# Batch norm over a matmul: the weight's first blocks loaded as two pairs, and chunk 0 multiplied in two passes over half of k

## The chip, the cores and the metric

One core of a Trainium2 chip runs the kernel. The core has five engines with an instruction queue each: TensorE (PE; its weight loads are shown apart as PEld), VectorE (DVE), ScalarE (ACT), GpSimd (POOL) and SyncE (SP). DMA transfers are issued by POOL and SP and are carried out by 16 DMA engines. The metric is the time on the device of one execution in microseconds (us); less is better.

## The reference

```python
x: (16, 512, 1024) float32;  weight: (1024, 768) float32;  gamma, beta: (768,)
y = np.matmul(x, weight)
mean = np.mean(y, axis=(0, 1), keepdims=True)
var = np.var(y, axis=(0, 1), keepdims=True)
y_norm = (y - mean) / np.sqrt(var + eps)
return (gamma * y_norm + beta).astype(np.float32)
```

Mean and variance go over all 8192 rows of y, so a column's output can be written only when that column is known for every row.

## The kernel before

**Tiling.** The 8192 rows of x are 16 chunks of 512 rows (`CH`, index c). k (1024) is cut into `JW` = 4 blocks (index jw 0 to 3), each of 2 x 128 in the contraction (index e). The 768 columns are 6 tiles of 128 (nt). The first two tiles (`GA` = 2, 256 columns) are computed by rows: x is the stationary operand and w moves ("rows", `rows_unit`, `mm_rows`, line 493). The other four are computed by columns: w is stationary and x moves ("columns", `col_unit`, `mm`, line 558).

**Loading.** POOL issues all loads of x and w, with a cast from float32 to bfloat16. One load of x (`load_x`, line 392) is four DMAs, one for each quarter of k; chunks 0 and 1 are loaded in halves of 256 rows (four DMAs of 128 KB, as they land), later chunks whole (four of 256 KB). One load of w (`load_w`, line 383) is four DMAs too, each for 32 of the 128 partitions, of the blocks jw to jw1: 96 KB for one block, 192 KB for two. A DMA from POOL takes one of eight lanes in turn, and its issue waits until the lane's previous DMA has landed. Before the loop SP reads a few bytes of w's block 0 (line 345).

**Turning x.** x arrives with rows along the partitions' free side in 32 x 32 blocks, and VectorE transposes it (`turn_x`, line 421; line 414 for the chunks in `SINGLE`). For chunk 0 each half of 256 rows is turned in two steps, first for the blocks 0 and 1 of k, then for 2 and 3; the other chunks in one step for each half.

**Order of the work.** The kernel makes a list of tasks with due times (`t` for loads, `clock[0]` for TensorE) and estimated durations for each engine. `arrange` (line 122) then simulates the engines, the DMA lanes and the buffers with these estimates, and fixes in which order each engine's instructions stand. So a change of an estimate or of one task can change the order on all engines. The list of the first loads is at line 426; the estimate for a w load is at line 437.

**TensorE's start.** `wake` (line 570) is work that computes nothing that is used. `wake(WAKE)` is eight float32 matmuls of width 512 and `SMALL` = 22 small bfloat16 matmuls of width 128 (line 577); `wake(FILL)` is `FILL` = 2 of the float32 ones (line 574). `part(q0, q1, jws)` (line 757) does rows and columns of chunk 0 for the half-chunks q0 to q1 and the blocks jws of k. What is done before the change, in this order: the first idle work; the first half-chunk with block 0; two idle matmuls; the second half-chunk with block 0; both halves with block 1; then both with the blocks 2 and 3, the rows by `rows_unit` and the columns by `col_unit` (lines 768 to 771). After that chunk 1 and the following chunks come with all of k at once. The sums go on in PSUM from one part to the next: two banks for rows, four for columns.

**After that.** Up to about 57 us TensorE does rows and columns of the chunks 1 to 3; then rows almost alone up to about 96 us, the rest of the first two column tiles (line 798) up to 106 us, and the columns of nt 2 to 5 of the remaining chunks until 190 us. ScalarE squares a rows' result (line 642) and copies it (line 655), VectorE (line 645) and POOL or VectorE (line 649) add up sums and squares. Normalized output is stored by SP from about 105 us on.

Of the kernel before, what the change touches and what calls it, by code (L numbers as in the profile page):

```python
# [227 lines left out]
def kernel(  # L228
# [27 lines left out]
    JW = KQ // 64  # L256
    PIECES = ((0,QR),(QR,QR))
    WAKE = 8
    FILL = 2
    SMALL = 22  # L260
    TOUCH = 1
    EARLY = 4
    SHORT = 2
# [27 lines left out]
    def seq(bi):  # L291

        ins = bi.ins
        prev = last.get(ins.engine)
        if prev is not None:
            tc.add_manual_dep(
                ins, prev,
                mybir.DependencyInfo(mybir.DependencyClass.NoSync, mybir.DependencyReason.DATA),
                reason="order",
            )  # L300
        last[ins.engine] = ins.name
        return bi
# [48 lines left out]
    def task(prio, engines, emit, deps=(), lock=False, **kw):  # L351
        t = Task(prio, engines, emit, deps, **kw)
        t.lock = lock
        tasks.append(t)
        return t

    def dve(occ):
        return {"DVE": (occ, occ + 0.09)}

    def act(occ):  # L360
        return {"ACT": (occ, occ + 0.11)}
# [14 lines left out]
    w_ready, x_ready, x_slot, plain, last_loads = {}, {}, {}, {}, []  # L376

    def load_w(jw, jw1):
        def emit(eng):
            rows = weight.rearrange("(i jw c e) n -> i c jw (e n)", i=4, jw=JW, e=2)  # L380
            dst = w_sb.rearrange("p jw e n -> p jw (e n)")
            for i in range(4):
                seq(nc.gpsimd.dma_start(dst[32 * i:32 * i + 32, jw:jw1], rows[i, :, jw:jw1]))
        return emit

    def load_x(m0, rows, slot):
        def emit(eng):
            x_bf = piece(slot).bitcast(bf16).rearrange("p (t k) -> p t k", k=KQ)
            slot.tile = x_bf
            src = x_flat[m0:m0 + rows].rearrange("(t r) k -> r t k", r=32)  # L390
            for i in range(4):
                bi = seq(nc.gpsimd.dma_start(x_bf[32 * i:32 * i + 32], src[:, :, KQ * i:KQ * (i + 1)]))  # L392
            slot.loader.ins = bi.ins
        return emit
# [8 lines left out]
    def turn_x(xslot, slot, m0, t0, jw0, jw1, new, rows=QR):  # L403
        def emit(eng):
            single = m0 // CH in SINGLE
            if new:
                xT_sb = xtpool.tile([P, JW, 2, CH] if single else [P, JW, CH, 2], bf16, tag="xT")
                slot.tile = xT_sb
            half, row = divmod((m0 + 32 * t0) % CH, QR)
            if single:  # L410
                src = xslot.tile[:, t0:t0 + rows // 32].rearrange("p t (jw c e) -> p t jw e c", jw=JW, e=2)
                dst = slot.tile[:, :, :, half * QR + row:half * QR + row + rows]
                dst = dst.rearrange("p jw e (t r) -> p t jw e r", r=32)
                seq(nc.vector.transpose(dst[:, :, jw0:jw1], src[:, :, jw0:jw1]))  # L414
                return
            src = xslot.tile[:, t0:t0 + rows // 32].rearrange("p t k -> p (t k)").bitcast(f32)
            src = src.rearrange("p (t jw c) -> p t jw c", jw=JW, c=32)
            dst = slot.tile.rearrange("p jw m e -> p (jw m e)").bitcast(f32)
            dst = dst.rearrange("p (jw q t r) -> p q t jw r", jw=JW, q=QPC, r=32)
            dst = dst[:, half, row // 32:(row + rows) // 32, jw0:jw1]  # L420
            seq(nc.vector.transpose(dst, src[:, :, jw0:jw1]))  # L421
        return emit

    for c in range(C):
        x_slot[c] = Slot(xts)
    order = [("x", 0), ("w", 0, 1)] + [("x", 1), ("w", 1, 2), ("w", 2, 4)]
    order += [("x", q) for q in range(2, SHORT * QPC)] + [("c", c) for c in range(SHORT, C - 1)]
    at = M - CH
    for rows in (CH-P,P):
# [2 lines left out]
    t = 1.0  # L432
    affine = None
    for kind, n, *n1 in order:
        if kind == "w":
            took = 4 * 192 * 4 * (n1[0] - n) / 4 * PER_KB * 1.024
            w_ready[n] = task(t, {"POOL": (2.0, 2.0)}, load_w(n, *n1), dma=took)
            w_ready[n].count = 4
            t += 2.1 * (n1[0] - n)
            if n1[0] == JW:  # L440
                idt = task(t, {"POOL": (0.6, 0.6)}, lambda eng: make_identity(nc, ident))
                task(t, act(0.25), lambda eng: seq(nc.scalar.copy(ident32, ident)), [idt])
            continue
        rows = n1[0] if kind == "p" else QR if kind == "x" else CH
        m0 = n if kind == "p" else n * rows
        if m0 == M // 2:
            affine = task(t, {"SP": (5.0, 7.0)}, load_affine, [x_ready[m0 // CH - 3, 0, JW]])
        slot = Slot(rings, rows // 32 * KQ // 2)
        load = task(
            t, {"POOL": (2.68 * rows / CH, 2.68 * rows / CH)}, load_x(m0, rows, slot), dma=rows * K * 4 / 1024 * PER_KB * 1.024,  # L450
            takes=[slot])
        load.count = 4
        slot.loader = load
        last_loads.append(load)
        t += 2.7 * rows / QR
        for i in range(rows // QR):
            c, q = divmod(m0 // QR + i, QPC)
            for j0, j1 in ((0, JW // 2), (JW // 2, JW)) if m0 < CH else ((0, JW),):
                new = q == 0 and j0 == 0
                x_ready[c, q, j1] = task(  # L460
                    -1000 + t, dve((2.2 if c in SINGLE else 1.16) * (j1 - j0) / JW + 0.02),
                    turn_x(slot, x_slot[c], m0, i * QR // 32, j0, j1, new), [load],
                    uses=[slot] if new else [slot, x_slot[c]], takes=[x_slot[c]] if new else [])
                if not new:
                    x_ready[c, q, j1].deps.append(x_ready[c, 0, JW // 2 if m0 < CH else JW])
            x_ready.setdefault((c, q, JW // 2), x_ready[c, q, JW])
        if rows % QR:
            t0 = rows // QR * QR // 32
            m1 = m0 + 32 * t0
            c, q = divmod(m1 // QR, QPC)  # L470
            x_ready["tile", m1 // P] = task(
                -1000 + t, dve(0.63), turn_x(slot, x_slot[c], m0, t0, 0, JW, False, P),
                [load, x_ready[c, 0, JW]], uses=[slot, x_slot[c]])
            x_ready[c, q, JW] = x_ready[c, q, JW // 2] = x_ready["tile", m1 // P]
# [95 lines left out]
    def wake(count, slot):  # L570
        def emit(eng):
            idle_ps = psum.tile([P, CH], f32, tag="b")
            for _ in range(count):
                seq(nc.tensor.matmul(idle_ps, idle_sb[:, 0:P], idle_sb, start=True, stop=True))  # L574
            small = idle_sb[:, 0:P // 2].bitcast(bf16)
            for _ in range(SMALL if count == WAKE else 0):
                seq(nc.tensor.matmul(idle_ps[:, 0:P], small, small, start=True, stop=True))
        return emit
# [5 lines left out]
    def pe_task(occ, emit, deps, key=None, **kw):  # L584
        t = task(clock[0], pe(occ), emit, deps, **kw)
        t.after = begun.get(key)
        begun[key] = t if key else None
        emit.task = t
        clock[0] += occ
        return t  # L590
# [7 lines left out]
    def rows_unit(c, ts, jws=range(JW)):  # L598
        key = "row", c, ts[0]
        slot = bank_of.setdefault(key, None) or Slot(banks)  # L600
        bank_of[key] = slot
        kw = {"takes": [slot], "uses": [x_slot[c]]} if jws[0] == 0 else {"uses": [slot, x_slot[c]]}
        h = ts[0] * P // QR
        t = pe_task(0.873 * len(ts) * len(jws) / JW, mm_rows(c, ts, list(jws), slot),
                    waits(jws, c, h, h + 1), key, **kw)
        if jws[-1] == JW - 1:
            rows_stats(c, ts, slot, t)
        return t
# [148 lines left out]
    def part(q0, q1, jws):  # L757
        for h in range(q0, q1):
            rows_unit(0, [2 * h, 2 * h + 1], jws)
        for nt in range(GA, NT):  # L760
            col_unit(nt, 0, jws, q0, q1)

    part(0, 1, [0])
    fill_slot = Slot(banks)
    pe_task(0.87 * FILL, wake(FILL, fill_slot), [w_ready[0]], takes=[fill_slot])
    part(1, 2, [0])
    part(0, 2, [1])
    for h in range(2):
        rows_unit(0, [2 * h, 2 * h + 1], [2, 3])
    for nt in range(GA, NT):  # L770
# [500 lines left out]
    for c, r0, rows in ends:  # L1271
        due = E + 2.0 + 0.6 * c
        n = max(rows // CH, 1)
# [30 lines left out]
    order = arrange(tasks, turns)  # L1304
# [39 lines left out]
```

## Time and profile before

| | us |
|---|---|
| runs (three) | 208.77, 208.78, 208.35; median 208.77 |
| span of the profiled execution, first to last instruction | 206.5 |
| TensorE busy in it | 191.4 (93 %) |
| VectorE busy | 156.3 (76 %) |
| ScalarE busy | 139.8 (68 %) |
| POOL busy | 132.0 (64 %) |
| granted clock of TensorE, mean | 0.985 |

The profile page lists a busy time for each engine, then the span in slices, then the chain of work that ended last: from the last instruction it is followed back, at each step to what released it. On the chain, lines 558 and 493 (columns and rows) have 51 % and 23 % of the span, loads of x 5 % and loads of w 3 %. TensorE's busy time is no measure of how full it is, since matmuls overlap; more is told by what it waited for. The profiled execution's own time is not listed apart from its span; the runs' median is 2.27 us above the span.

A line of the timeline is: start, length, engine, line of the kernel, operation, output<-inputs, shape, how many, and in brackets the idle time before it and what ended it. A line of the windows is: the stretch, its length, then busy time and number of instructions of PE, PEld, DVE, ACT and POOL, the granted clock, the DMA engines' share and what they wrote in GB/s. A line of the waits is: who waited <- for whom, us in total, times, longest.

### The profile page before, as it was taken

How to read it: one execution, taken by the hardware profiler on the slowest of the kernel's cores; microseconds unless marked ns; L12 is line 12 of the kernel's file. 1: busy time of each engine (PE TensorE's matmuls, PEld its weight loads, DVE VectorE, ACT ScalarE, POOL GpSimd, SP SyncE). 2: the span in 40 equal slices, each digit the busy share in tenths (PEclk: the TensorE clock that was granted, in tenths of full speed). 3: DMA queues.
4: the chain of work that ended last, by engine and by line, in shares of the span. 5: the costliest groups of instructions: out<-in, count | busy, mean ns of one | idle time of the engine just before them, and what ended most of it. 6: DMA issues, size and time to landing. Idle time of an engine off the chain costs nothing.

```text
span 206.5 us, 3506 instructions
## 1 busy us (share of the span) xinstructions
PE 191.4 (93%) x1211; PEld 116.3 (56%) x1226; DVE 156.3 (76%) x238; ACT 139.8 (68%) x248; POOL 132.0 (64%) x148
## 2 busy tenths in 40 slices
PE   7998999999999999999999999999999999996900
PEld 3465564747488888777875444444444445553600
DVE  4220779999999999968989998977999648947900
ACT  2000560369989999998978767997376776866950
POOL 7877964877488999999304999599954440440000
PEclk9999999999999999999999999999999999999995
DMA  5999999999999999999676898999999999999898
GB/s 55 169 168 193 192 196 196 196 198 197 190 193 197 197 197 195 196 197 195 110 120 199 311 339 307 267 350 307 315 317 245 291 325 308 274 341 347 254 347 243
DMA packets 98497, 48.73 MB, mean 236 GB/s; under 512 B 24240, under 2 KB 97968, under 8 KB 98480
## 3 DMA queue, kind: packets, MB, share of 16 engines
q0 software_dynamic: 34688, 18.36, 65.1%
q1 hardware_dynamic: 63792, 30.16, 52.8%
q8 instruction: 9, 0.15, 0.3%
q14 instruction: 8, 0.07, 0.1%
HBM read 36.71 MB, written 25.17 MB: 300 GB/s over the span
## 4 chain that ended last, share of the span: by engine, by line
PE 82%; DMA 8%; ACT 3%; issue 1%; POOL 1%; DVE 1%; ACTq 0%; POOLq 0%
PE y_ps L558 51%; PE y_ps L493 23%; DMA ring<-in_x_dram 5%; PE y_ps L798 4%; ACT o_sb L1293 3%; DMA w_sb<-in_weight_dram 3%; PE o_ps L1028 2%; PE a_ps L887 1%; POOL ring L392 1%; PE y_ps L736 1%; PE o_ps L1058 0%; ACTq L1339 0%; PE tot_ps L855 0%; DVE fin L743 0%; ACT y_sb L746 0%
## 5 line engine op out<-in xcount | busy, mean ns | idle before, releaser
L558 PEld LDWEIGHTS <-w_sb 128*128 128x128 bf16 x512 | 49.7, 97 | 57.4
L558 PE MATMUL y_ps<-x_pl,w_sb 128*128 128x512 bf16 x256 | 60.5, 379 | 0.3
L392 POOL DMA_DIRECT2D ring<-in_x_dram x76 | 47.5, 630 | 13.0 <-DVE xT_sb L414 5.0
L558 PE MATMUL y_ps<-xT_sb,w_sb 128*128 128x512 bf16 (+1 forms) x241 | 55.1, 376 | 0.4
L493 PE MATMUL y_ps<-w_sb,xT_sb 128*128 128x256 bf16 x448 | 50.7, 273 | 0.6 <-DMA w_sb<-in_weight_dram 0.6
L493 PEld LDWEIGHTS <-xT_sb 128*128 128x128 bf16 x448 | 43.6, 98 | 8.3 <-issue 1.7
L421 DVE STREAM_TRANSPOSE xT_sb<-ring 128x1024 f32<-128x1024 f32 (+1 forms) x29 | 31.2, 1111 | 12.4 <-DMA ring<-in_x_dram 12.2
L694 DVE BATCH_NORM_STATS2 stats<-y_ps 128x6 f32<-128x512 f32 x46 | 30.9, 687 | 12.7 <-PE y_ps L558 12.5
L698 ACT CAST y_sb<-y_ps 128x512 bf16<-128x512 f32 x51 | 29.4, 590 | 14.5 <-DVE stats L694 12.4
L926 POOL TENSOR_TENSOR ring<-ring,sum 128x1024 f32<-128x1024 f32 (+1 forms) x11 | 23.7, 2193 | 14.6 <-DVE ring L921 14.5
L649 POOL TENSOR_TENSOR sum<-sum,sq_sb 128x512 f32<-128x512 f32 x21 | 26.9, 1281 | 3.2 <-ACT sq_sb L642 2.1
L642 ACT ACTIVATE sq_sb<-y_ps 128x512 f32<-128x512 f32 x28 | 16.3, 607 | 18.0 <-PE y_ps L493 17.1
L645 DVE TENSOR_TENSOR sum<-y_ps,sum 128x512 f32<-128x512 f32 x28 | 18.9, 675 | 9.1 <-ACT sq_sb L642 7.8
L530 ACT COPY x_pl<-xT_sb 128x1024 bf16<-128x1024 bf16 x24 | 24.4, 1052 | 1.7 <-DVE xT_sb L421 1.7
L655 ACT CAST y_sb<-y_ps 128x512 bf16<-128x512 f32 x28 | 16.0, 599 | 7.8 <-DVE sum L645 7.6
L530 POOL COPY x_pl<-xT_sb 128x1024 bf16<-128x1024 bf16 x15 | 16.1, 1108 | 8.0 <-DVE x_pl L530 5.2
L921 DVE TENSOR_TENSOR ring<-y_sb,a_ps 128x1024 f32<-128x1024 bf16 (+1 forms) x16 | 16.7, 1080 | 0.3 <-DMA out_dram<-ring 0.3
L1139 POOL TENSOR_TENSOR ring<-ring,sum 128x1024 f32<-128x1024 f32 x4 | 9.6, 2412 | 11.0 <-DVE ring L1135 11.0
L1193 ACT CAST ring<-ring 128x1024 f32<-128x1024 bf16 x15 | 15.7, 1049 | 1.0 <-DMA ring<-y_sb 1.0
L1028 PE MATMUL o_ps<-ident,y_sb 128*128 128x128 bf16 x104 | 14.2, 221 | 2.2 <-DVE y_sb L1280 2.0
L414 DVE STREAM_TRANSPOSE xT_sb<-ring 128x2048 bf16<-128x2048 bf16 x6 | 13.5, 2289 | 0.2 <-DMA ring<-in_x_dram 0.2
L574 PE MATMUL idle_ps<-idle_sb 128*128 128x512 f32 x20 | 11.2, 717 | 1.5 <-DVE idle_sb L314 1.5
(97 smaller groups left out, 155.0 us busy)
## 6 DMA issues: line engine op xcount, KB each, us to landing
out_dram<-ring SPq DMA_DIRECT2D x38, 512.0 KB, 3.7
ring<-in_x_dram POOLq DMA_DIRECT2D x52, 256.0 KB, 8.8
out_dram<-o_sb SPq DMA_DIRECT2D x6, 512.0 KB, 4.9
ring<-in_x_dram POOLq DMA_DIRECT2D x16, 128.0 KB, 5.3
out_dram<-ring SPq DMA_DIRECT2D x4, 256.0 KB, 3.0
w_sb<-in_weight_dram POOLq DMA_DIRECT2D x8, 96.0 KB, 5.1
w_sb<-in_weight_dram POOLq DMA_DIRECT2D x4, 192.0 KB, 5.9
ring<-in_x_dram POOLq DMA_DIRECT2D x4, 192.0 KB, 8.1
```

The lines of the kernel that those rows point to most:

```text
L392: bi = seq(nc.gpsimd.dma_start(x_bf[32 * i:32 * i + 32], src[:, :, KQ * i:KQ * (i + 1)]))
L421: seq(nc.vector.transpose(dst, src[:, :, jw0:jw1]))
L493: seq(nc.tensor.matmul(y_ps[:, s], x_of(c, jw, e, t * P, (t + 1) * P), w_sb[:, jw, e, 0:NA], start=(s == 0 and jw == 0 and e == 0), stop=( ...
L530: seq(nc.scalar.copy(dst, pairs) if eng == "ACT" else ENG[eng].tensor_copy(dst, pairs))
L558: seq(nc.tensor.matmul(y_ps, w_sb[:, jw, e, nt * P:(nt + 1) * P], moving(c, jw, e, q0 * QR, q1 * QR, parted), start=(jw == 0 and e == 0 an ...
L645: seq(nc.vector.tensor_add(sum1, slot.tile[:, 0:n], sum1))
L649: seq(ENG[eng].tensor_add(acc, acc, state["sq"][:, 0:n]))
L694: seq(nc.vector.bn_stats(dst, slot.tile))
L698: seq(nc.scalar.copy(y(nt, c), slot.tile))
L921: seq(nc.vector.tensor_mul(slot.o, y_row[c].y[:, s0:s1], aff[0][:, None, :].to_broadcast([P, n, NA])))
L926: seq(ENG[eng].tensor_add(slot.o, slot.o, row[:, None, :].to_broadcast([P, n, NA])))
L1028: seq(nc.tensor.transpose(dst, src, ident))
```

## The change

```diff
-    FILL = 2
-    SMALL = 22
+    FILL = 1
+    SMALL = 34
...
-    order = [("x", 0), ("w", 0, 1)] + [("x", 1), ("w", 1, 2), ("w", 2, 4)]
+    order = [("x", 0), ("w", 0, 2), ("x", 1), ("w", 2, 4)]
...
-            w_ready[n] = task(t, {"POOL": (2.0, 2.0)}, load_w(n, *n1), dma=took)
+            w_ready[n] = task(t, {"POOL": (2.14, 2.14)}, load_w(n, *n1), dma=took)
...
-    part(0, 1, [0])
+    part(0, 1, [0, 1])
     fill_slot = Slot(banks)
     pe_task(0.87 * FILL, wake(FILL, fill_slot), [w_ready[0]], takes=[fill_slot])
-    part(1, 2, [0])
-    part(0, 2, [1])
+    part(1, 2, [0, 1])
```

w comes in two loads of four DMAs instead of three: the blocks 0 and 1 between the two halves of chunk 0, and the blocks 2 and 3 after them as before. Chunk 0 then takes two passes over k for its first half of k: the first half-chunk with the blocks 0 and 1, and the second half-chunk with the same; the blocks 2 and 3 follow for both, as before. The columns of block 1, once eight matmuls of width 512, become sixteen of width 256. Twelve small idle matmuls are added before the first pass, and one of the two idle matmuls between the passes is gone. The planner's estimate of POOL's time for a w load goes from 2.0 to 2.14 us.

In the order that the planner then fixes, TensorE's instructions after chunk 0 and SP's are as before. On POOL, VectorE and ScalarE some instructions of the row phase stand otherwise: one add of squares goes from POOL to VectorE, POOL has one add more ahead of the loads of chunks 10 and 11, VectorE turns chunk 9 before an add instead of after it, and ScalarE has squares and copies of three rows' results in another order.

## Prediction
> **What bounds the kernel now.** I read the chain of waits first, then the waits of TensorE, then its timeline in the stage that the diff touches, then the rates of the DMA engines. The chain's columns are start, length, what.
>
> ```profile
> 8.65 4.67 DMA ring<-in_x_dram
> 13.32 0.28 issue
> 13.61 6.00 DMA w_sb<-in_weight_dram
> 19.61 0.14 issue
> 19.74 1.91 PE y_ps L493 x16
> 21.65 3.62 PE y_ps L558 x16
> 25.26 3.67 PE y_ps L493 x32
> ```
>
> Up to 19.74 us the chain is loading: the last quarter of x's second half-chunk lands at 13.32, and frees the lane on which the last quarter of w's blocks 2 and 3 is issued (13.61); that lands at 19.61. From 19.74 on the chain is TensorE, almost without a break. TensorE's own waits (total, times, longest) say the same:
>
> ```profile
> PE o_ps L1028 <- DVE y_sb L1280: 2.0, 1, 2.0
> PE idle_ps L574 <- DVE idle_sb L314: 1.5, 1, 1.5
> PE y_ps L493 <- DMA w_sb<-in_weight_dram: 0.6, 1, 0.6
> ```
>
> Of these, the first is the closing stage and the second the start; between lies one wait, on w. So the change is worth what it moves the moment 19.74, provided that nothing later takes it back.
>
> The stage itself on TensorE:
>
> ```profile
> 10.67 1.39 PE L577 MATMUL idle_ps<-idle_sb 128*128 128x128 bf16 x22
> 12.33 1.07 PE L558 MATMUL y_ps<-xT_sb,w_sb 128*128 128x256 bf16 x8
> 13.24 1.88 PE L574 MATMUL idle_ps<-idle_sb 128*128 128x512 f32 x4
> 16.30 1.03 PE L493 MATMUL y_ps<-w_sb,xT_sb 128*128 128x256 bf16 x8
> 17.40 1.74 PE L558 MATMUL y_ps<-xT_sb,w_sb 128*128 128x512 bf16 x7
> ```
>
> Start to start this gives prices: a small idle matmul (11.89 - 10.67) / 22 = 0.0555 us; a row matmul 0.109 (16 from 19.74 to 21.48); a 512-wide column matmul 0.2255 (16 from 21.48 to 25.10); a 256-wide column matmul (13.24 - 12.33) / 8 = 0.114; an idle matmul of line 574 two passes, together (14.96 - 13.24) / 2 = 0.86.
>
> **The loads, piece by piece.** The view of the two loading lines, asked issue by issue, gives issue and time to landing. x's first half lands until 8.37. Block 0 of w (issued from 3.73, 5.0 to 5.1 each) lands at 8.8 to 10.26, 0.48 apart. x's second half lands at 10.9, 11.6, 12.3, 13.32; block 1 at 14.4, 14.9, 15.3, 15.8; the pair 2 and 3 at 16.8, 17.7, 18.7, 19.61. In step, a quarter of one w block takes 0.48, of x 0.68, of a pair 0.94: 4 x 0.48 + 4 x 0.68 + 4 x 0.48 + 4 x 0.94 = 10.32, so from 8.37 the end would be 18.69. It was 19.61. The missing 0.92 lies in two steps: x's last quarter (1.03 instead of 0.68) and block 1's first (1.07 instead of 0.48). The rates by window (last number, GB/s) show the same dip:
>
> ```profile
> 12.00:15.00 3.00, 3.00 (x19) 1.78 (x16) 1.30 (x2) 0.00 (x0) 1.81 (x4) 1.00 1.04 155
> 15.00:19.60 4.60, 4.08 (x28) 2.57 (x27) 0.00 (x0) 0.00 (x0) 3.70 (x7) 1.00 1.14 197
> 30.00:80.00 50.00, 49.89 (x367) 35.81 (x367) 48.09 (x54) 37.47 (x60) 39.39 (x50) 1.00 1.49 196
> ```
>
> The late quarters also had a short time from issue to landing (4.7, 5.2); the pair's had 5.6 to 6.1 and all came on time. So the queue may have been too shallow there. It may also be the reads of a fresh block of w that were slow; the page can't say.
>
> **The change, part by part.**
>
> *POOL's queue.* Eight issues of single blocks (0.50 each) become four of a pair (0.53, as the pair's from 11.21): the first w load ends at 3.73 + 4 x 0.53 = 5.85 instead of 5.71. Behind it stand the two identity operations (0.23, 0.31) and x's second half. Its first issue slips from 5.84 to 6.0, the second likewise; the third and fourth wait for landings of x's first half (7.66, 8.37) and stay at 7.94 and 8.65. Cost nothing: x's data now stand behind a pair that lands until 12.1. The second pair takes the lanes of the first, so it is issued some 0.28 after each of its landings, 9.6 to 12.4. Behind these waits on POOL stand only the loads of chunk 1, whose data follow the pair's anyway.
>
> *Landings.* 8.37 + 4 x 0.94 = 12.13 for blocks 0 and 1; + 4 x 0.68 = 14.85 for x; + 4 x 0.94 = 18.61 for blocks 2 and 3. Each of these last eight would have about 6.2 from issue to landing. Best case 1.00 earlier than 19.61; worst of the plain cases, the 0.92 recurs and it is 0.08 earlier. I take the best, since leads of 5.6 and more came on time in this stage, and keep both.
>
> [...]
>
> *TensorE.* Twelve more small idle matmuls: real work begins at 10.67 + 34 x 0.0555 = 12.56, not 11.89; w is there at 12.13. First pass, 8 rows and 16 columns: 0.87 + 1.82 = 2.69, to 15.25. One idle matmul less: 0.86, to 16.11. x's second half is turned for k's first half by 14.85 + 0.13 + 0.65 + 0.1 = 15.73, so no wait. Second pass 2.69, to 18.80. In all the same work: 16 columns of 0.114 stand for 8 of 0.2255. The pair is usable 0.13 after landing, 18.74. So blocks 2 and 3 begin at 18.80 instead of 19.74, with the same 32 matmuls still to do: **0.94 earlier**; 0.05 with the late pieces.
>
> *Later stages.* x's loads run at 196 GB/s without a pause, so the whole stream moves with the pair, 1.00. It must, for late in the row phase both meet (chunk 12):
>
> ```profile
> 84.91 2.37 DVE L421 STREAM_TRANSPOSE xT_sb<-ring 128x1024 f32<-128x1024 f32 x2 [0.23 <-DMA ring<-in_x_dram]
> 86.25 0.75 PEld L493 LDWEIGHTS <-xT_sb 128*128 128x128 bf16 x6
> ```
>
> The first transpose ends 1.25 after 84.91, at 86.16; TensorE loads it at 86.25. It can gain 0.09 more than the loads do and no more. The built order also moves work behind this: on POOL one more add of squares (1.28) stands ahead of the loads of chunks 10 and 11, on VectorE one more (0.68) between the transposes of chunks 9 and 10. Chunk 11 is issued at 68.27 with 7.1 to landing; 5.8 is left, and 5.1 to 5.6 was enough for the last x loads. VectorE's is hidden by the waits of 0.23 (chunk 12) and 1.59 (chunk 13) on loads; uncovered it costs 0.68 - 0.23 = 0.45. I take nothing for both, and 0.19 for slips of the kind already there: 32 row matmuls of chunk 1 took 3.67, of chunk 2 3.49.
>
> *Sum.* 0.94 - 0.19 = 0.75. The profiled span is 206.5, to become 205.75; the median of the runs, 208.77, lies 2.27 above the span: **208.0**.
>
> **The rivals.**
>
> *The lateness comes again once* (a fresh block of w is slow to read, wherever it stands). For: the dip ends with block 1. Against: block 0 came on time behind x. Gain 0.05 to 0.4, about **208.6**.
>
> *It comes twice, and the kernel is slower.* Place: the landing of either pair; price 0.92 each. Then blocks 2 and 3 land at 18.61 + 1.84 = 20.45, TensorE starts 0.84 later: **209.6**. It decides from 1.00 of lateness in all. For: the step to block 1 is the only one where w came late, and both pairs now begin with such a step. Against: the pair at 15 to 19.6 ran at 197 GB/s.
>
> *TensorE's clock falls back*, since fewer idle matmuls stand between. That there are two speeds is seen in the first idle matmuls, at equal granted clock:
>
> ```profile
> 5.07 0.33 PEld L574 LDWEIGHTS idle_ps<-idle_sb 128*128 128x128 f32 x1 [0.52 <-issue]
> 5.92 0.22 PEld L574 LDWEIGHTS idle_ps<-idle_sb 128*128 128x128 f32 x1 [0.52 <-issue]
> 6.38 0.19 PEld L574 LDWEIGHTS idle_ps<-idle_sb 128*128 128x128 f32 x1 [0.24 <-issue]
> ```
>
> 0.85 from one to the next, then 0.43, after 4.4 us of work. At half speed for as long, half the work is lost: +2.2, about **210.2**. Against: the pause of 0.6 before 19.74 left the row matmuls at 0.109, and the worst new pause is under 1 us (x late by 0.9: 16.1 to 16.6, and another before the second pair). [...]
>
> **How the numbers follow.** Forecast 0.52 (own range 207.7 to 208.45), late once 0.25, late twice 0.14, clock 0.05, the moved adds 0.04 (208.5 to 209.5). The first two and the near edge of the third make the range 207.6 to 209.0. The measurement tells 0.2 %, 0.42 us: faster means below 208.35. Faster: 0.9 of the forecast and a tenth of late once, 0.50. Slower: late twice, clock, most of the moved adds and a little of the rest, 0.25. Same: 0.25.
>
> **What would show it.** Right: the wait on w before line 493 shrinks from 0.60 to under 0.1 and ends by 18.9; the rate from 12 to 15 us is near 195; the second pair lands by 18.7; x of chunk 12 is turned about 1 us earlier. Wrong: a rate near 155 again at some place before 16 us (late once, or twice); row matmuls at twice 0.109 after a pause (clock); an early start whose gain is gone at chunk 12, with a new wait of TensorE on line 421 (moved adds).

## The result, and the profile after

| | before | after |
|---|---|---|
| median of 10 runs each (lowest to highest), us | 207.88 (207.39 to 208.78) | 209.12 (208.78 to 209.85) |
| span of the profiled execution, us | 206.5 | 207.1 |

The ratio after to before is 1.005, 95 % interval 1.0031 to 1.0068: the changed kernel is slower by about 1 us. The three runs that the prediction started from (208.35 to 208.78) are among the ten of the kernel before, and among its four slowest; the other seven have a median of 207.79. The kernel before also differs from one group of experiments to the next (207.94 to 208.30), so from here on a run is compared by its ratio to the runs of the kernel before that stand beside it.

At chunk 0 nearly all came as predicted. The chain of waits of the changed kernel (start, length, what), from the small idle matmuls to the blocks 2 and 3:

```profile
11.02 1.90 PE idle_ps L577 x34
12.92 0.87 PE y_ps L493 x8
13.80 1.81 PE y_ps L558 x16
15.61 0.86 PE idle_ps L574 x2
16.47 0.87 PE y_ps L493 x8
17.34 1.81 PE y_ps L558 x16
19.15 1.75 PE y_ps L493 x16
```

No load stands on it any more; TensorE goes from one piece into the next and begins the blocks 2 and 3 at 19.15 on this chain. A piece of the chain starts only where the one before it ends; by the timeline, which the prediction used, the first pass starts at 12.76 and the blocks 2 and 3 at 18.99. Before, they started at 19.74 in both views. The waits of TensorE are down to the start and the closing stage:

```profile
PE o_ps L1027 <- DVE y_sb L1279: 2.0, 1, 2.0
PE idle_ps L574 <- DVE idle_sb L314: 1.5, 1, 1.5
```

The windows over the loading (the last number is GB/s) have no dip: 206 where it was 155.

```profile
12.00:15.00 3.00, 3.00 (x38) 2.70 (x36) 0.00 (x0) 0.00 (x0) 2.30 (x5) 1.00 1.35 206
15.00:18.60 3.60, 3.60 (x29) 2.67 (x27) 1.30 (x2) 0.00 (x0) 2.31 (x5) 1.00 1.14 200
```

Nor is the gain lost on the way. Chunk 12 is turned at 84.24 (before 84.91), its rows start at 85.54 (86.47), and the chains reach the last matmuls of y, line 736, and the first normalization of the last column tile with 0.91 in hand. Before, then after:

```profile
187.04 1.83 PE y_ps L736 x16
...
190.49 0.36 DVE y_sb L1280
```

```profile
186.13 1.83 PE y_ps L736 x16
...
189.58 0.36 DVE y_sb L1279
```

From that normalization to the end of the span (206.54 before, 207.13 after) it takes 16.06 us before and 17.56 after; this stretch is called the closing stage below. So 0.91 is gained by 189.6 us, and 1.50 is lost in the closing stage, which the change does not touch. What ends the span there are the stores. Windows over the last of them, before:

```profile
204.00:204.50 0.50, 0.00 (x0) 0.00 (x0) 0.00 (x0) 0.00 (x0) 0.00 (x0) 0.50 1.15 344
204.50:205.00 0.50, 0.00 (x0) 0.00 (x0) 0.00 (x0) 0.00 (x0) 0.00 (x0) 0.50 1.10 330
205.00:205.50 0.50, 0.00 (x0) 0.00 (x0) 0.00 (x0) 0.00 (x0) 0.00 (x0) 0.50 0.07 18
205.50:206.00 0.50, 0.00 (x0) 0.00 (x0) 0.00 (x0) 0.00 (x0) 0.00 (x0) 0.50 0.00 0
```

and after:

```profile
204.00:204.50 0.50, 0.00 (x0) 0.00 (x0) 0.00 (x0) 0.00 (x0) 0.00 (x0) 0.50 0.58 170
204.50:205.00 0.50, 0.00 (x0) 0.00 (x0) 0.00 (x0) 0.00 (x0) 0.00 (x0) 0.50 0.07 22
205.00:205.50 0.50, 0.00 (x0) 0.00 (x0) 0.00 (x0) 0.00 (x0) 0.00 (x0) 0.50 0.07 22
205.50:206.00 0.50, 0.00 (x0) 0.00 (x0) 0.00 (x0) 0.00 (x0) 0.00 (x0) 0.50 0.05 15
```

The stores run at about 345 GB/s on 16 DMA engines, which is 21.6 for one. After the change the full rate ends earlier, at about 204.25, but then 22 GB/s go on for more than 1.5 us, with a mean share of 0.07, about 1/16: that is the share of one DMA engine that has still to finish while fifteen are done. Before, this tail was under half a microsecond.

The page's list of DMA queues names what is new. Before, then after (packets, MB, share of 16 engines):

```profile
q8 instruction: 9, 0.15, 0.3%
```

```profile
q8 instruction: 10, 0.16, 0.3%
```

The instructions of the program are themselves brought by DMA, 0.16 MB / 10 = 16 KB at a time, and the changed kernel needs one such transfer more. The queues of the changed kernel in the window from 196 to 197.5 us:

```profile
q1 hardware_dynamic: 984, 0.50, 110.8%
q8 instruction: 1, 0.02, 4.0%
```

The tenth transfer lies among the last stores and takes 0.040 x 16 x 1.5 = 0.96 us of one DMA engine. The view does not name the engine of a transfer; that it is the one that finishes late is inferred. Before, that window holds none; its ninth and last came at 179.5. The program that grew is TensorE's: the page counts 1226 weight loads before and 1244 after, each with its matmul (12 small idle matmuls and 8 columns more, 2 less of the float32 idle matmul, which takes two: the timeline before has four for the two of `FILL`). That is 36 instructions more on top of 2452.

### The profile page after: what moved, and what is told of

It is laid out like the page before. It is cut to its first block, busy times and chain, and to the rows that moved or that the text cites. A ratio compares the mean times of both kernels' runs of the same rounds, so it can differ in the third digit from the quotient of the medians.

```text
span 207.1 us, 3552 instructions
## 1 busy us (share of the span) xinstructions
PE 192.1 (93%) x1244; PEld 119.0 (57%) x1244; DVE 157.2 (76%) x239; ACT 139.7 (67%) x248; POOL 129.1 (62%) x143
## 4 chain that ended last, share of the span: by engine, by line
PE 91%; ACT 3%; DVE 1%; ACTq 0%; issue 0%
PE y_ps L558 53%; PE y_ps L493 24%; PE idle_ps L574 5%; PE y_ps L797 4%; ACT o_sb L1292 2%; PE o_ps L1027 2%; PE a_ps L886 1%; PE idle_ps L577 1%; PE y_ps L736 1%; PE o_ps L1057 0%; ACTq L1338 0%; PE tot_ps L854 0%; DVE idle_sb L314 0%; DVE fin L743 0%; ACT y_sb L746 0%
## 5 line engine op out<-in xcount | busy, mean ns | idle before, releaser
L558 PEld LDWEIGHTS <-w_sb 128*128 128x128 bf16 x520 | 50.4, 97 | 56.9
L558 PE MATMUL y_ps<-x_pl,w_sb 128*128 128x512 bf16 x264 | 61.3, 379 | 0.0
L558 PE MATMUL y_ps<-xT_sb,w_sb 128*128 128x512 bf16 (+1 forms) x256 | 55.7, 370 | 0.0
L649 POOL TENSOR_TENSOR sum<-sum,sq_sb 128x512 f32<-128x512 f32 x20 | 25.6, 1278 | 3.4 <-ACT sq_sb L642 2.4
L574 PE MATMUL idle_ps<-idle_sb 128*128 128x512 f32 x18 | 10.6, 743 | 1.5 <-DVE idle_sb L314 1.5
```

The costliest lines, as they stand in the source:

```text
L558: seq(nc.tensor.matmul(y_ps, w_sb[:, jw, e, nt * P:(nt + 1) * P], moving(c, jw, e, q0 * QR, q1 * QR, parted), start=(jw == 0 and e == 0 an ...
L649: seq(ENG[eng].tensor_add(acc, acc, state["sq"][:, 0:n]))
```

## The experiments

Three theories for the lost 1.5 us. Each result below is the median of the run, its ratio to the kernel before with the 95 % interval in brackets, and what its profile shows; a transfer is one of the program's instructions (queue q8).

- **F**, the fetch: the 36 added instructions bring about a tenth transfer of TensorE's program, it falls into the closing stores, and one DMA engine finishes late.
- **O**, the order: the planner's other order on POOL, VectorE and ScalarE shifts the closing stage.
- **C**, the clock: TensorE's granted clock falls to half for some microseconds in the closing stage of the changed kernel (0.50 from 192 to 194 us, 0.74 on average from 192 to 196; before, 1.00 in both).

**e1: the changed kernel with fewer small idle matmuls.**

```diff
-    SMALL = 34
+    SMALL = 28
```

> The changed kernel with SMALL = 28 instead of 34: six small idle matmuls (12 instructions of TensorE) fewer, all else in the same order on every engine. Theory F (instruction fetch): the changed kernel's program for TensorE has just outgrown a multiple of 16 KB, so a tenth transfer of instructions falls into the closing stores (196.3 us) and holds up one DMA engine; with 12 instructions fewer the page lists 9 instruction transfers, none after 185 us, and the time is 206.8 to 207.4 us against 207.9 before (the 0.9 us won at chunk 0 stays). Rival C (clock): the closing stage is longer because TensorE is put to half clock in it; it reaches that stage at the same moment here, so the time stays near 209.1. Rival O (order): the moved adds and transposes cost it; same order here, so 209.1 as well.

Measured: 207.94 us, ratio to the kernel before 0.9995 (0.9978 to 1.0013); closing stage 15.87 us; nine transfers within the span, the next one after its end (207.3). Twelve instructions fewer take the loss away and leave the new loading, the two passes and the other engines' order in place. The clock was halved in this closing stage too (0.57 on average from 192 to 196), against C. The time is above the 206.8 to 207.4 expected and shows no clear gain, so part of the 0.94 of the prediction was missing: in the profiled execution x's first half landed at 9.10 (8.37 in the profile before) and the second pair at 19.31.

**e2 and e3: the kernel before, with more and with fewer small idle matmuls.** Both have one idle matmul less between the passes, and with it the same order on the other engines; they differ in 16 small idle matmuls alone.

```diff
-    FILL = 2
-    SMALL = 22
+    FILL = 1
+    SMALL = 46
```

```diff
-    FILL = 2
-    SMALL = 22
+    FILL = 1
+    SMALL = 30
```

> The kernel before with SMALL = 46 and FILL = 1: w still in three loads and chunk 0 in three passes; 24 small idle matmuls more and one float32 idle matmul less (about the same idle time, 47 instructions of TensorE more), and the planner then makes the same order on VectorE and ScalarE as in the changed kernel. TensorE still waits for blocks 2 and 3 of w, so chunk 0 ends as before. Theory F: 10 instruction transfers, the last after 190 us, and 1.0 to 1.4 us slower than before, 208.9 to 209.3. Rival C: the clock drop depends on an earlier arrival, which isn't there: 207.9. Rival O: slower, about 209.

> As the run with SMALL = 46, but SMALL = 30 (15 instructions of TensorE more than before); order on VectorE, ScalarE, POOL and SP the same as there. Theory F: 9 instruction transfers as before, time 207.9 (207.6 to 208.2), about 1.1 us less than with 46. Rival O: as slow as the run with 46, about 209. Rival C: both 207.9.

Measured: e2 210.47 us, 1.011 (1.0089 to 1.0131), more than the 208.9 to 209.3 expected; e3 208.56 us, 1.0009 (0.9994 to 1.0024). Their queue lines on the page, e2 and then e3:

```profile
q8 instruction: 10, 0.16, 0.3%
```

```profile
q8 instruction: 9, 0.15, 0.3%
```

The spans are 208.9 and 206.5. The longer idle block lets the last matmuls of y begin at 187.36 instead of 186.66, which is 0.70 of the 2.4; the other 1.7 lies in the closing stage, 18.08 against 16.38. e2's tenth transfer stood at 195.8. The windows of e2 show the same lone engine at the end:

```profile
205.00:205.50 0.50, 0.00 (x0) 0.00 (x0) 0.00 (x0) 0.00 (x0) 0.00 (x0) 0.50 1.15 349
205.50:206.00 0.50, 0.00 (x0) 0.00 (x0) 0.00 (x0) 0.00 (x0) 0.00 (x0) 0.50 0.26 73
206.00:207.00 1.00, 0.00 (x0) 0.00 (x0) 0.00 (x0) 0.00 (x0) 0.00 (x0) 0.50 0.07 22
```

So the loss is made without the change's loads and passes (e2), and taken away without altering the order (e3 against e2, e1 against the changed kernel): O falls.

**e4: the changed kernel with its small idle matmuls as a few wide ones,** about the same idle time in fewer instructions.

```diff
-    SMALL = 34
+    SMALL = 2
+    WIDE = 8
...
+            wide = idle_sb[:, 0:CH // 2].bitcast(bf16)
+            for _ in range(WIDE if count == WAKE else 0):
+                seq(nc.tensor.matmul(idle_ps, small, wide, start=True, stop=True))
```

> The changed kernel with its 34 small idle matmuls replaced by eight of width 512 and two small ones: the same 1.9 us of idle work in 48 instructions fewer, so that real work begins at the same time. Theory F: 9 instruction transfers, 206.8 to 207.4. Rivals C and O: 209.1. A rival by which the beginning of the first pass matters (SMALL = 28 begins 0.33 us sooner) would have this one at 209.1 and the one with 28 below it.

Measured: 207.56 us, 0.9971 (0.996 to 0.9982), a little above the times expected, and 0.3 % faster than the kernel before; nine transfers; closing stage 16.1 us. TensorE began the blocks 2 and 3 at 18.78 (timeline). In this execution the clock was halved in the closing stage as in the changed kernel's (the third number from the end, 0.78 against 0.74 below), and the stage was not longer: C falls. The window from 192 to 196, e4 and then the changed kernel:

```profile
192.00:196.00 4.00, 3.51 (x47) 3.33 (x44) 2.84 (x9) 3.79 (x6) 0.00 (x0) 0.78 1.03 310
```

```profile
192.00:196.00 4.00, 3.71 (x48) 3.54 (x46) 3.02 (x10) 3.79 (x5) 0.00 (x0) 0.74 1.01 303
```

**e5: the changed kernel with SMALL = 32,** four instructions fewer.

```diff
-    SMALL = 34
+    SMALL = 32
```

> The changed kernel with SMALL = 32 instead of 34: two idle matmuls of 0.0555 us fewer, four instructions of TensorE; all other orders the same. In the changed kernel the tenth instruction transfer began when all but some three of TensorE's recorded instructions had begun. Theory F: with four fewer that point is reached only by the closing instructions of the program, so the tenth transfer is gone from the stores (absent, or after 205 us), and two small matmuls are worth 1.0 to 1.5 us: about 0.5 us under before. Rivals C and O, or a theory by which the load of many small idle matmuls counts: within 0.2 us of the changed kernel.

Measured: 208.98 us, 1.0041 (1.002 to 1.0062); ten transfers, the tenth at 196.4; closing stage 17.35. The expectation missed: the four were not enough to be rid of the transfer. The core of F stands, for the transfer and the loss are still there together; the limit lies between e1's 2 x 1238 = 2476 instructions of weight loads and matmuls and e5's 2 x 1242 = 2484.

**e6: the kernel before with wide idle matmuls** (as e4, with WIDE = 5), to see what they bring without the change.

> The kernel before with its 22 small idle matmuls replaced by five of width 512 and two small ones: the same 1.2 us of idle work in 30 instructions fewer. It asks whether the changed kernel with wide idle matmuls (0.6 us under before) won by fewer instructions or by the loads and passes. Theory F, by which only a transfer in the closing stores costs: the same as before within 0.2 us, 9 instruction transfers or fewer. Rival (each instruction saved counts): 0.4 to 0.6 us under before.

Measured: 208.53 us, 1.0017 (0.9999 to 1.0034); nine transfers; closing stage 16.1. They bring nothing by themselves, and nothing like the 0.4 to 0.6 us of the rival.

**e7: the kernel before with the two pairs alone,** without the two passes and with its idle matmuls.

```diff
-    order = [("x", 0), ("w", 0, 1)] + [("x", 1), ("w", 1, 2), ("w", 2, 4)]
+    order = [("x", 0), ("w", 0, 2), ("x", 1), ("w", 2, 4)]
...
-            w_ready[n] = task(t, {"POOL": (2.0, 2.0)}, load_w(n, *n1), dma=took)
+            w_ready[n] = task(t, {"POOL": (2.14, 2.14)}, load_w(n, *n1), dma=took)
```

> The kernel before with w in two pairs alone: three passes, FILL = 2 and SMALL = 22 as before, so TensorE has as many instructions as before. 9 instruction transfers expected by every theory. By the steps of the prediction: the first half-chunk waits for blocks 0 and 1 (12.2 to 12.9 us), 1.35 of work, 1.72 of idle matmuls, the second half-chunk not before 15.7, 1.35 and then 2.84 for block 1: blocks 2 and 3 are begun at about 19.9 although they land at 18.7. So 0 to 0.3 us slower than before: the loads gain nothing without the passes. Rival (the loads alone bring the gain): 0.5 us faster than before.

Measured: 207.98 us, 0.9987 (0.9969 to 1.0004); nine transfers; closing stage 15.99. The pairs alone cost nothing and bring at most little. (The planner's order on VectorE, ScalarE and POOL is a third one in this run.) w was there at 18.77, but TensorE began the blocks 2 and 3 only at 19.52 (timeline): its idle block and the passes set that moment here, not the load.

**e8: the changed kernel again.** No edit.

> The changed kernel once more, on the same chip as the three others. Theory F: the tenth instruction transfer is again near 196 us, and the stretch from the first normalization of the last column tile to the end is 17.5 us, against about 16 in all runs without it; 1.0 to 1.5 us over the run with SMALL = 32.

Measured: 209.1 us, 1.004 (1.0023 to 1.0056); the tenth transfer at 197.7; closing stage 17.27. Transfer and loss are there again; the distance of 1.0 to 1.5 us to e5 is not, since e5 kept its transfer.

**e9 and e11: more instructions, so that the tenth transfer comes sooner.** 90 small idle matmuls in place of six float32 ones add 78 weight loads and as many matmuls, 156 instructions; the planner keeps its estimate, so that the order elsewhere is the changed kernel's.

```diff
-    WAKE = 8
+    WAKE = 2
...
-    SMALL = 34
+    SMALL = 124
...
-    task(1.0, pe(0.87 * WAKE), wake(WAKE, wake_slot), takes=[wake_slot])
+    task(1.0, pe(0.87 * 8), wake(WAKE, wake_slot), takes=[wake_slot])
```

> The changed kernel with 90 more small idle matmuls ahead of chunk 0 (WAKE=2, SMALL=124), the order on the other engines as in the changed kernel; TensorE's program is some 180 instructions longer. Theory F (the tenth transfer of TensorE's program falls into the closing stores and costs there): the tenth transfer comes 10 us or so sooner, at about 184 to 188 us, before the closing stores begin; the stage from the first normalization of the last tile to the end takes about 16 us again (15.9 to 16.4, not 17.3 to 18.1), and the time is 207.2 to 208.2 us, unless the 90 idle matmuls last past the landing of x, which would show as a later first pass. Rival (what costs is the number of instructions, wherever their transfers fall): 209.1 us or more, with a closing stage of 17.3 us or more.

> The version with 90 more small idle matmuls once more, now on the same chip and side by side with the changed kernel (the next run). Theory F: a closing stage of about 16 us and a median at least 0.5 us below that of the changed kernel beside it. Rival (the number of instructions costs by itself): a median equal to that of the changed kernel or above it.

**e12: the changed kernel a third time,** beside e11.

> The changed kernel, unchanged, beside the version with 90 more small idle matmuls. Theory F: ratio to the kernel before 1.002 to 1.007, ten transfers of TensorE's program with the tenth at 195 to 198 us, a closing stage of 17.2 to 18.1 us. If the ratio lies under 1.002 here, the loss depends on the chip and not on the place of the transfer alone.

Measured: e9 208.2 us, 1.0002 (0.998 to 1.0024), the tenth transfer at 186.3, closing stage 15.91. Side by side on one chip, e11 took 207.73 us, ratio 1.000 (0.9977 to 1.0024), and e12 209.26 us, 1.0066 (1.0053 to 1.0078). Both have ten transfers. In e11 the tenth came at 184.0 and the closing stage took 15.94 (from 189.75); in e12 it came at 197.8 and the stage took 17.34 (from 189.78). The last windows, e11 and then e12:

```profile
204.00:204.50 0.50, 0.00 (x0) 0.00 (x0) 0.00 (x0) 0.00 (x0) 0.00 (x0) 0.50 0.59 173
204.50:205.00 0.50, 0.00 (x0) 0.00 (x0) 0.00 (x0) 0.00 (x0) 0.00 (x0) 0.50 0.00 0
```

```profile
204.00:204.50 0.50, 0.00 (x0) 0.00 (x0) 0.00 (x0) 0.00 (x0) 0.00 (x0) 0.50 0.67 198
204.50:205.00 0.50, 0.00 (x0) 0.00 (x0) 0.00 (x0) 0.00 (x0) 0.00 (x0) 0.50 0.07 22
205.00:205.50 0.50, 0.00 (x0) 0.00 (x0) 0.00 (x0) 0.00 (x0) 0.00 (x0) 0.50 0.07 22
```

So it is neither the number of instructions nor that of their transfers that costs: e11 has more instructions than any other version, as many transfers as e12, and no loss. The place of the tenth costs, 1.5 us. At 184 the DMA engines are as full of stores as at 197 (343 GB/s from 183.5 to 189 us in e11, 344 from 194 to 199 in e12); but there a pause of the stores follows, in which a late engine could catch up. That this is why is a reading of the rates; no run takes the pause away. In e11's rates from 180 to 209 us (40 slices of 0.725 us), the pause is the 16th slice, at 190.9 to 191.6:

```profile
GB/s 345 347 346 350 341 357 329 338 345 349 350 335 348 347 325 38 197 256 344 345 347 347 347 348 345 350 346 347 347 347 345 349 346 155 0 0 0 11 0 0
```

e12 also speaks against C once more: the granted clock was 1.00 up to 199 us, and the loss was there.

**e10: a version to beat both.** As e4 with WIDE = 6, and the idle matmul between the two passes left out; its time stays in the planner's clock.

```diff
-    fill_slot = Slot(banks)
-    pe_task(0.87 * FILL, wake(FILL, fill_slot), [w_ready[0]], takes=[fill_slot])
+    clock[0] += 0.87
```

> The changed kernel with its 34 small idle matmuls as 6 wide ones and 2 small ones, and without the wide idle matmul between the two passes: some 50 instructions fewer on TensorE than the changed kernel. Theory F: nine transfers, a closing stage of about 16 us and 207.2 to 207.8 us, ratio to the kernel before 0.995 to 0.998, like the version with 8 wide ones. Rival (the idle matmuls hold the clock up between the passes): half clock behind chunk 0 for some microseconds, 208.5 us or more.

Measured: 207.7 us, 0.9966 (0.9945 to 0.9986); nine transfers; closing stage 15.88; the granted clock stayed at 1.00 behind chunk 0. With e4 it is the fastest here, below the kernel before; the two can't be told apart. The idle matmul between the passes isn't needed.

Taken together: of the fourteen profiles, the five with a transfer behind that pause and before the end of the stores (the changed kernel, e2, e5, e8, e12) have a closing stage of 17.27 to 18.08 us, the nine others one of 15.87 to 16.39.

## Why the prediction was wrong

- *What bounds the kernel, and the proviso.* It made the change worth what it moves the moment 19.74, "provided that nothing later takes it back". The first half held (0.91 was still there at 189.6 us), the proviso didn't.
- *The step that failed* is the cost of the part "TensorE". There the twelve added idle matmuls and the sixteen columns in place of eight were priced by their time on TensorE alone, and the sum has no term for the stage behind 188 us. The runs put a term of +1.5 us in this place: 36 more instructions bring a transfer of TensorE's program into the closing stores. The profiled span missed its forecast by 1.38 (207.13 for 205.75): by this term less what TensorE gained on the way beyond the forecast (0.91 for 0.75). This term was not among the rivals: the slower one put the loss at the landing of the pairs, and both pairs came in step. The page of the kernel before does list the queue, 9 transfers of 16 KB (in its trace the last is at 179.5 us); the prediction does not compare them with the growth of the program.
- *POOL's queue and the landings* were right: the second pair landed at 18.66, for 18.61 predicted, with no dip. *TensorE's prices* were right too (0.87, 1.81 and 0.86 on the chain). By the timeline the first pass began at 12.76 instead of 12.56, since the idle block's small matmuls began at 10.86 instead of 10.67, and so the blocks 2 and 3 at 18.99 instead of 18.80: 0.75 earlier than before, not 0.94.
- *The 0.94 as a gain* was too large for a usual run. It was taken against one execution of the kernel before, in which w landed at 19.61. With the loads as before it landed at 18.74 and 18.80 in e6 and e2, and at 19.04 in e3; as pairs at 18.48 to 19.76 in ten executions (half of them under 18.77). Two things stand behind these numbers. Counted from the landing of x's first half, in step the last w takes 10.32 as before and 10.24 as pairs (a quarter of one block, 96 KB, took 0.48 in the profile before, one of a pair, 192 KB, 0.94, so the merging alone is worth 4 x (2 x 0.48 - 0.94) = 0.08); the four executions with the loads as before took 10.77 to 11.24, of the ten with pairs seven took 10.21 to 10.46 and three 10.66 to 11.37. So some of the dip stood in each of the four, and the pairs take most of it away in most executions. But x's first half itself landed at 7.92 to 8.37 in the four and at 7.74 to 9.19 in the ten, and moves all behind it; whether the pairs behind it are a reason is open. So the 19.61 of one execution was in part its luck. The prediction left open whether the queue or the reads were at fault; the runs leave it open too.
- *Later stages.* The 0.19 for slips was not needed: chunk 1's 32 row matmuls took 3.49 after the change (24.35 to 27.84), without the slip that the profile before has there, so TensorE's lead went from 0.75 to 0.93; it was 0.93 at chunk 12 and 0.91 at the last matmuls. But x's stream did not move as a whole. The last piece of chunk 10 landed 1.18 earlier than before (72.91 for 74.09), that of chunk 11 only 0.64 (78.78 for 79.42), that of chunk 12 0.67. The loads of chunk 11, for which the prediction took nothing, were issued only 0.11 earlier (68.16 for 68.27), behind the moved add; that the add is the reason is not tested. TensorE did not lose by it, for it had more room at chunk 12 than the 0.09 that the prediction read: x came 0.67 earlier there, and its rows started 0.93 earlier.
- *Small figures.* By its own terms the late case leaves 0.08 (19.53 + 0.13 against 19.74), not 0.05; the slip 3.67 - 3.49 is 0.18, and a 512-wide column matmul 3.62 / 16 = 0.226. None of them changes the forecast.
- *The forecast in ratio* was 208.0 / 208.77 = 0.9963. The versions that make the change without the late transfer have 0.9971 and 0.9966 where wide idle matmuls replace the small ones (e4, e10), and 0.9995 to 1.0002 where they don't (e1, e9, e11). Why these differ by some 0.6 us isn't settled; e6 shows that wide idle matmuls bring nothing without the change. So that e4 and e10 meet the forecast does not confirm its 0.94.
- *The clock* did not fall back behind chunk 0, as predicted: eight row matmuls took 0.87 in both passes, 0.109 each as before, and in e10, without the idle matmul between them, the sixteen at the start of the blocks 2 and 3 took 1.91 on the chain, as in the kernel before; the granted clock was 1.00. What such a fall would cost no run shows; the 2.2 is the prediction's estimate from the first idle matmuls.

## What to carry to other kernels

Instructions added here had a cost beside their engine's time: with 36 more on TensorE the closing stage took 17.56 us instead of 16.06. The program came in by DMA beside the data, 16 KB at a time, so compare the number of instruction transfers on the two pages, and look where the last ones fall. In this closing stage, which stores at 345 GB/s up to the end, one more transfer cost 1.5 us; fewer instructions (e1, e4, e10), or a transfer moved ahead of a pause (e11), took it away. And a gain that consists of one execution's late landing should be weighed against other executions before it is counted in full.

## What the runs showed of the hardware

TensorE's program came in pieces of 16 KB here. Between two transfers the trace of the changed kernel has 192 to 298 TensorE instructions, 251 on average. Of the first nine transfers no run here shows a cost. The tenth cost 1.5 us (e12 against e11), and not by a wait of TensorE: in the changed kernel 2514 of its 2517 recorded instructions had begun when that transfer started. What ended later was the stores, on one DMA engine, by the share of 0.07 in the last windows.

The lone engine's tail is longer than the transfer: some 1.6 us at 22 GB/s, 35 KB, for a transfer of 16 KB that took 0.96. No run here shows how the engine divided its time between the transfer and the stores, and why the tail is longer stays open.

TensorE's first idle matmuls start 0.85 us apart at first and 0.43 apart later. The closer spacing begins at 6.38 us in the profile before and at 6.57 in that of the changed kernel, and the small idle matmuls behind them at 10.67 and 10.86. It differs from one execution to the next: up to the small ones the same sixteen passes took 9.53 us on the chain of the changed kernel and 10.12 on that of e2. The first pass began at 12.76 in the profile of the changed kernel and at 12.30 in e8, the same kernel.
